# A hybrid pooling and HGRN2 layer on one core: channel-major prompt tokens, broadcast roots, projection banks in turn from two pools, and later final stores

## The chip, the cores and the metric

The kernel runs on one NeuronCore of a Trainium2 chip. The core has a matrix engine (TensorE, PE in the profile; its weight loads are the row PEld), a vector engine (VectorE, DVE), an engine for activations, copies and casts (ScalarE, ACT), a general engine (GpSimd, POOL) and a queue engine (SyncE, SP) that issues most of the transfers. Each engine runs its own instructions in order, and semaphores order the engines against each other. The matrix engine writes into PSUM, eight banks of 128 rows by 512 float32 values; everything else lies in SBUF, 128 partitions wide. Sixteen transfer engines move data between the chip's memory and SBUF.

The metric is the device time of one execution in microseconds (us). Three runs of the kernel before had a median of 2188.99 us.

## The reference

One layer of a streaming encoder is computed for two groups of requests with the same weights: 2048 new tokens (the prompt) and 32 tokens of a running stream (the sample), each of 1024 channels. In short, with B = 1:

```python
h = rmsnorm(x, g_pre_mix)                  # x * rsqrt(mean(x*x) + 1e-6) * g, over 1024 channels
z = h @ w_in                               # 1024 -> 2560
u, zq, zf, zi, zg = split(z, 5 x 512)
y_pool = windows of u over 2/4/8/16 frames, minus u, times w_pool per group, times pool_scale
q, f = silu(zq), lb + (1 - lb) * sigmoid(zf)
o, S1 = hgrn_run(S0, q, k=(1 - lb) * sigmoid(-zf), v=zi, log(f))   # 4 heads of 128, per token exact
y_hg = rmsnorm(o, g_hg_norm) * silu(zg)
x = x + rmsnorm(concat(y_pool, y_hg) @ w_out, g_post_mix)
h2 = rmsnorm(x, g_pre_ffn)
x = x + rmsnorm((silu(h2 @ w_gate) * (h2 @ w_up)) @ w_down, g_post_ffn)   # 2816 hidden
```

It returns the new x of both groups, the last 15 pooling inputs and the last matrix states. All inputs are float32. The kernel keeps nearly that precision by writing an operand as a rounded high part and a rest (hi and lo) and adding three products: hi*hi, hi*lo and lo*hi.

## The kernel before

The prompt is worked in two halves of 1024 tokens (A, then B; B also carries the 32 sample tokens). A half is two blocks of 512 tokens (`tg` 0 and 1), and a block is four tiles of 128 tokens. Per half the order on TensorE, written out by hand (`manual_schedule` for PE), is:

- `values`: the 512 value columns of `w_in` for each token block, 8 channel tiles x 4 token tiles x 3 products of 512 columns, so 96 products a block
- `head_products`: for each of four heads the columns f, q and g, each for the two blocks of 512 tokens, 24 products a block; behind them as background tasks the recurrence (`hgrn`)
- `pool_products`: four pooling groups
- `project`: `w_out`, for each block two column halves (`dh`), each into four PSUM banks
- `gate_up`: gate and up products in a seven-product scheme, results written to memory as hi and lo (`hd`)

Behind both halves follows `down`: six groups of hidden columns, each over eight units (half, token position), each unit seven products out of tiles that SP fetches from `hd` one unit ahead, summed into `acc`.

The other engines' instructions are ordered by a planner that knows estimated durations. Background tasks (`Task`) are advanced by `poll`, which is called between products and compares each task's due time with a running count of estimated TensorE time (`Pace`). Weights come through a stream: `want` lists them, `ahead` loads raw tiles (two items in front) and splits them into hi and lo (`split`: ACT casts, DVE subtracts), `take` hands out the next.

SBUF tiles come from two rotating pools, 39 tiles of 4 KB a partition and 22 of 2 KB; PSUM has a pool `mm` of four banks and a pool `ax` of four.

The places around the change:

- **Input.** `body` loads the first two token tiles, a block of constants and five small vectors (as rows, turned by one transpose, lines 102 to 131). `front_norm` loads token tiles (128 tokens x 1024 channels), forms the mean square on ACT (`sumsq`), the root on POOL (`rstd_of`, line 295, with `pow`), scales the tile on DVE (lines 459 and 469), and `to_channels` (lines 306 to 326) transposes each 128 x 128 piece on TensorE into an `ax` bank, from which ACT writes hi and DVE lo of `hT`. For A's first block this runs per pair of token tiles. For B it starts while A's `gate_up` ends.
- **Projection.** Each `dh` takes three `mm` banks and one `ax` bank (line 875). DVE multiplies them by the gain and ACT sums their squares. Meanwhile `post` of the block before works on the result: residual, second norm, transposes by `to_raw` (line 328) in `ax` banks, and forms on ACT and DVE.
- **Final stores.** In the last group of `down`, a finished token tile is scaled, then an accumulating transfer issued by POOL adds the residual (line 1397), and SP stores the tile (line 1398); this store is put at least six slots (products of one unit and position) after the accumulating transfer in the program. The last unit's two tiles are added on DVE instead and stored by lines 1392 and 1393, on SP and, for the last piece, ACT's queue.

## Time and profile before

| what | value |
|---|---|
| median of three runs | 2188.99 us (2187.97 to 2190.52) |
| the profiled execution | 2187.68 us |
| its span, first to last instruction | 2185.9 us |
| mean granted TensorE clock | 0.997 |
| TensorE busy | 2143.7 us, 98% of the span |
| DVE, ACT, POOL busy | 1414.3, 817.5 and 282.4 us |
| moved by transfers | 315.13 MB, 144 GB/s |

The profile is of one execution. A row of busy time names the line of the kernel, the engine, the operation, the tiles written and read, and the count; "L184" is the helper that issues every ordinary matmul. The table of waits gives who waited, for whom, the total in us, how often, and the longest. The table of stretches gives, for each interval of the span, every engine's busy time with its instructions in brackets, the share of the clock granted to TensorE (1.00 is full), the mean busy share of the 16 transfer engines (it can exceed 1 where packets of several queues overlap), and GB/s. A row of the timeline starts with start and duration; a bracket at its end says how long the engine had been idle and what ended that. Matmuls overlap in the pipeline, so the distance between their starts, not their duration, is what one costs.

### The profile page before, as it was taken

What the parts mean: (1) busy time and instruction counts of PE and PEld (TensorE: products, weight loads), DVE (VectorE), ACT (ScalarE), POOL (GpSimd) and SP (SyncE); (2) the same over time, 40 slices, a digit from 0 to 9 for tenths busy, and PEclk for the clock granted to TensorE, in tenths of its full rate; (3) what the DMA queues carried; (4) which work ended last, traced back from release to release, by engine and by line L of the source; (5) the groups of instructions that cost most, each with busy time, mean ns of one, the idle gap of its engine ahead of it and who ended that gap; (6) DMA issues with size and microseconds to landing.
All of it is one profiled execution on the core that took longest, in us unless ns stands there. A gap on an engine that the chain in (4) does not pass through costs nothing.

```text
span 2185.9 us, 34308 instructions
## 1 busy us (share of the span) xinstructions
PE 2143.7 (98%) x13293; PEld 1712.5 (78%) x13293; DVE 1414.3 (65%) x2309; ACT 817.5 (37%) x1586; POOL 282.4 (13%) x383
## 2 busy tenths in 40 slices
PE   7999999999999999999999999999999999999996
PEld 5878878788888888777777778888888777877785
DVE  6356665697776778365574687766666756566585
ACT  6233234554444456132323564444444521011032
POOL 1033201100000001023220120000000210110033
PEclk9999999999999999999999999999999999999999
DMA  6110043425555558111014524544454797777789
GB/s 221 39 31 21 21 145 131 149 82 169 162 148 151 155 164 268 43 44 34 15 32 146 180 86 125 159 141 140 135 145 140 228 327 200 220 223 206 203 226 308
DMA packets 385179, 315.13 MB, mean 144 GB/s; under 512 B 15701, under 2 KB 318058, under 8 KB 385017
## 3 DMA queue, kind: packets, MB, share of 16 engines
q1 hardware_dynamic: 382856, 305.34, 46.0%
q0 software_dynamic: 2016, 7.34, 1.7%
q8 instruction: 105, 1.72, 0.3%
q14 instruction: 58, 0.47, 0.1%
q10 hardware_dynamic: 144, 0.26, 0.0%
HBM read 214.51 MB, written 98.37 MB: 143 GB/s over the span
## 4 chain that ended last, share of the span: by engine, by line
PE 43%; DVE 3%; DMA 2%; ACT 1%; POOL 1%; issue 0%; SPq 0%; DVEq 0%; POOLq 0%; ACTq 0%
PE gx L184 10%; PE dx L184 10%; PE gy L184 6%; PE dy L184 5%; PE ops L184 4%; PE dz L184 2%; PE gz L184 2%; PE mmb L184 1%; DMA hst<-hdTrue 1%; PE gsps L184 1%; DVE acc L1360 1%; PE gw L184 1%; PE sacc L184 0%; PE zps L184 0%; PE pps L184 0%
## 5 line engine op out<-in xcount | busy, mean ns | idle before, releaser
L184 PE MATMUL gx<-fhi,wf 128*128 128x512 f32 x1376 | 448.5, 394 | 0.0
L184 PEld LDWEIGHTS gx<-fhi,wf 128*128 128x128 f32 x1376 | 258.7, 188 | 59.2 <-issue 1.0
L184 PE MATMUL gx<-flo,wf 128*128 128x512 f32 x688 | 270.1, 393 | 0.0
L184 PE MATMUL gy<-fhi,wf 128*128 128x512 f32 x704 | 234.0, 394 | 0.0
L184 PE MATMUL mmb<-hThi,whi 128*128 128x512 f32 x512 | 219.0, 428 | 0.0
L184 PE MATMUL dx<-dhi,hst 128*128 128x512 f32 x640 | 213.5, 394 | 0.5 <-DVE acc L1360 0.4
L184 PE MATMUL mmb<-hThi,wlo 128*128 128x512 f32 x512 | 201.4, 393 | 0.0
L184 PE MATMUL mmb<-hTlo,whi 128*128 128x512 f32 x512 | 201.2, 393 | 0.0
L1360 DVE TENSOR_TENSOR acc<-dx,acc 128x512 f32<-128x512 f32 x168 | 115.2, 689 | 77.9 <-PE dx L184 77.3
L1094 DVE TENSOR_TENSOR wf<-s,wf 128x512 fp32r<-128x512 f32 x176 | 120.5, 688 | 66.1 <-ACT wf L1089 63.5
L184 PEld LDWEIGHTS gy<-fhi,wf 128*128 128x128 f32 x704 | 132.3, 188 | 30.6 <-issue 0.5
L184 PEld LDWEIGHTS gx<-flo,wf 128*128 128x128 f32 x688 | 129.6, 188 | 28.3
L1089 ACT CAST wf<-s 128x512 fp32r<-128x512 f32 x176 | 108.4, 621 | 105.4 <-PE gy L184 34.7
L184 PEld LDWEIGHTS dx<-dhi,hst 128*128 128x128 f32 x640 | 120.8, 189 | 32.2 <-issue 3.6
L184 PE MATMUL gy<-flo,wf 128*128 128x512 f32 x352 | 138.2, 392 | 0.0
L184 PE MATMUL dx<-dlo,hst 128*128 128x512 f32 x320 | 125.9, 394 | 0.0
L1094 DVE TENSOR_TENSOR wf<-wraw,wf 128x512 fp32r<-128x512 f32 x132 | 89.7, 687 | 50.9 <-ACT wf L1089 50.8
L184 PE MATMUL dy<-dhi,hst 128*128 128x512 f32 x320 | 113.1, 394 | 4.8 <-DMA hst<-hdTrue 4.4
L184 PEld LDWEIGHTS mmb<-hThi,whi 128*128 128x128 f32 x512 | 96.3, 188 | 25.0 <-issue 6.4
L1089 ACT CAST wf<-wraw 128x512 fp32r<-128x512 f32 x132 | 80.9, 620 | 88.3 <-PE gz L184 23.8
L184 PEld LDWEIGHTS mmb<-hThi,wlo 128*128 128x128 f32 x512 | 96.1, 188 | 22.3
L184 PEld LDWEIGHTS mmb<-hTlo,whi 128*128 128x128 f32 x512 | 96.7, 189 | 18.3 <-issue 2.6
(312 smaller groups left out, 4115.1 us busy)
## 6 DMA issues: line engine op xcount, KB each, us to landing
hst<-hdFalse SPq DMA_DIRECT2D x140, 256.0 KB, 2.9
hst<-hdTrue SPq DMA_DIRECT2D x140, 256.0 KB, 3.4
wraw<-in_w_gate_dram SPq DMA_DIRECT2D x50, 512.0 KB, 4.0
wraw<-in_w_up_dram SPq DMA_DIRECT2D x50, 512.0 KB, 3.9
hdFalse<-hhi SPq DMA_DIRECT2D x77, 256.0 KB, 2.6
hdFalse<-hlo SPq DMA_DIRECT2D x77, 256.0 KB, 2.5
hdTrue<-hhi SPq DMA_DIRECT2D x77, 256.0 KB, 2.4
hdTrue<-hlo SPq DMA_DIRECT2D x77, 256.0 KB, 3.1
```

The source lines that it names most:

```text
L184: nc.tensor.matmul(out, l, r, start=start, stop=stop, skip_group_check=more)
L1089: nc.scalar.copy(wf[:, 0], getattr(M, src) if isinstance(src, str) else src)
L1094: nc.vector.tensor_tensor(wf[:, 1], getattr(M, src) if isinstance(src, str) else src, wf[:, 0].bitcast(F32), ALU.subtract)
L1360: nc.vector.tensor_tensor(dst, ps, dst, ALU.add)
```

## The change

The prompt is given to the kernel a second time, channel-major (`x_channels`, 1024 x 2048), prepared with the inputs. The five small vectors become 32 more columns of the constants, loaded alone on ACT's queue.

**Input, half A** (`first_values`, all engines in program order): channel tiles are loaded beside the weights. The first block's value products use unnormed channels (times the gain, as hi and lo), and the results are multiplied by each token's root afterwards. For the second block, token tiles are loaded only for the statistics; the roots of 128 tokens, put on a diagonal by POOL, are multiplied by a matrix of ones on TensorE, which gives a bank that holds each token's root in all partitions; DVE multiplies gain and roots into the channel tile, ACT writes hi, DVE lo (`scaled_channels`). The first block's `hT` is made in the same way at the end of `first_values`. The heads of A then take the second block first, and the first head works f and q block by block.

**Input, half B**: the mean squares come from token halves loaded during A's heads (`later_stats`), and channel tiles are scaled as above. Nothing is transposed at the input but the 32 sample tokens.

**Projection**: the first column half takes all its banks from `mm`, the second from `ax`; the transposes of `to_raw` use the pool that the projection does not (`turned`). B's second block keeps one bank of the other pool for the sample.

**Stores**: 14 slots of distance instead of 6.

```diff
-                for ap, r0, n in ((ins["g_pre_mix"], 0, 8), (ins["g_pre_ffn"], 8, 8), (ins["pool_scale"], 16, 4),
-                                  (ins["lb_logits"], 20, 8), (ins["g_hg_norm"], 28, 1)):
-                    nc.sync.dma_start(out=rows[r0:r0 + n, :], in_=ap.rearrange("a (k p) -> (a k) p", p=P))
+        nc.scalar.dma_start(out=cons[:, C_VEC:C_END], in_=cst[:, C_VEC:C_END])
...
+        x_t = ins["x_channels"].rearrange("(k p) t -> p k t", p=P)
...
+        nc.gpsimd.memset(ones, 1.0)
...
-        def to_channels(tiles, dst, gcol, col0, seen=None, which=()):
...
-                ps = axbank("tps")
+                ps = turned[0]("tps")
...
+            S.blocks = [(0, 512), (512, 1024)] if B else [(512, 1024), (0, 512)]
...
+        def channel_load(S, tg, k, n):
+            t0 = S.tok0 + tg * 512
+            nc.sync.dma_start(out=S.xT[tg][k // 2][:, k % 2:k % 2 + n], in_=x_t[:, k:k + n, t0:t0 + 512])
+
+        def token_tiles(S, tg):
+            S.xt[tg] = [ztile("xt", [P, D]) for _ in range(4)]
+            for i, xt in enumerate(S.xt[tg]):
                 r0 = S.tok0 + (tg * 4 + i) * P
                 nc.sync.dma_start(out=xt, in_=x_p[r0:r0 + P, :])
-                xs.append((xt, P))
-            if S.B and tg == 1:
+
+        def token_stats(S, tg):
+
+            S.rs[tg], S.dg[tg] = [], t2("dg", [P, 4, P])
+            for i, xt in enumerate(S.xt[tg]):
+                st = new_stat()
+                sumsq(xt, P, st[:, 0:1])
+                S.rs[tg].append(rstd_of(st, P))
+                nc.gpsimd.tensor_scalar(S.dg[tg][:, i], ident, S.rs[tg][i], None, ALU.mult)
+            S.xt[tg] = None
+
+        def later_stats(S):
+
+            st = S.st
+            for i in range(NCH):
+                for c in range(2):
+                    x = t2("xtl")
+                    r0 = S.tok0 + i * P
+                    nc.sync.dma_start(out=x, in_=x_p[r0:r0 + P, c * 512:c * 512 + 512])
+                    sumsq(x, P, st[:, 2 * i + c:2 * i + c + 1])
+                    del x
+                yield 20000.0
+            ev = st[:, 0:16].rearrange("p (i c) -> p i c", c=2)
+            nc.gpsimd.tensor_tensor(st[:, 16:24], ev[:, :, 0], ev[:, :, 1], ALU.add)
+            nc.gpsimd.tensor_scalar(st[:, 16:24], st[:, 16:24], 1.0 / D, EPS, ALU.mult, ALU.add)
+            nc.gpsimd.tensor_tensor(st[:, 24:32], st[:, 16:24], nhalf[:, 0:1].broadcast_to([P, NCH]), ALU.pow)
+            S.rs = [[st[:, 24 + 4 * tg + i:25 + 4 * tg + i] for i in range(4)] for tg in range(2)]
+
+        def scaled_channels(S, tg):
+            rb = axbank("rb")
+            for i in range(4):
+                mm(rb[:, i * P:(i + 1) * P], ones, S.dg[tg][:, i], True, True, 112.0)
+            if S.hT is None:
+                S.hT = [(xtile(f"hThi{k}"), xtile(f"hTlo{k}")) for k in range(KD)]
+            cs = slice(tg * 512, tg * 512 + 512)
+            yield 0.0
+            for k in range(0, KD, 2):
+                x = S.xT[tg][k // 2]
+                for i in range(2):
+                    nc.vector.scalar_tensor_tensor(x[:, i], x[:, i], g_pre[:, k + i:k + i + 1], rb, ALU.mult, ALU.mult)
+                    nc.scalar.copy(S.hT[k + i][0][:, cs], x[:, i])
+                for i in range(2):
+                    hi, lo = (t[:, cs] for t in S.hT[k + i])
+                    nc.vector.tensor_tensor(lo, x[:, i], hi.bitcast(F32), ALU.subtract)
+                S.seen[tg] = k + 2
+                if S.B and tg == 0 and k >= 4:
+                    ahead(Stream.used + k // 2 - 1)
+                yield 5000.0 if S.B and tg == 0 else 2800.0
+
...
+        def front_norm(S, tg):
...
+            channel_tiles(S, tg)
+            S.dg[tg] = t2("dg", [P, 4, P])
+            for i in range(4):
+                nc.gpsimd.tensor_scalar(S.dg[tg][:, i], ident, S.rs[tg][i], None, ALU.mult)
...
+            yield from scaled_channels(S, tg)
...
+        def first_values(S):
+
+
+            front_loads(S)
+            S.xT[0] = [ztile("xT", [P, 2, 512]) for _ in range(4)]
+            for kp in range(4):
+                channel_load(S, 0, 2 * kp, 2 if kp else 1)
+                raws(kp + 1)
+                if kp == 0:
+                    channel_load(S, 0, 1, 1)
+            nc.sync.dma_start(out=cons[:, 0:C_VEC], in_=cst[:, 0:C_VEC])
+            xg = {}
+
+            def unscaled(k):
+                x, c = S.xT[0][k // 2][:, k % 2], xtile("xg", [P, 2, 512])
+                nc.scalar.activation(c[:, 0], x, AF.Copy, scale=g_pre[:, k:k + 1])
+                nc.vector.scalar_tensor_tensor(c[:, 1], x, g_pre[:, k:k + 1], c[:, 0].bitcast(F32), ALU.mult, ALU.subtract)
+                xg[k] = c[:, 0], c[:, 1]
+
+            token_tiles(S, 1)
+            S.xT[1] = [ztile("xT", [P, 2, 512]) for _ in range(4)]
+            for kp in range(4):
+                channel_load(S, 1, 2 * kp, 2)
+                raws(kp + 5)
+            token_tiles(S, 0)
+            unscaled(0)
+            ahead(1)
+            unscaled(1)
+            pss = value_tiles(S)
+            for k in range(0, KD, 2):
+                _, hi, lo = take(0)
+                if k + 2 < KD:
+                    unscaled(k + 2)
+                    ahead(Stream.used + 1)
+                    unscaled(k + 3)
+                else:
+                    ahead(Stream.used + 1)
+                if k == 4:
+                    token_stats(S, 1)
+                for kk in range(2):
+                    ah, al = xg.pop(k + kk)
+                    for i in range(4):
+                        value_products(pss, i, ah, al, i * P, hi[kk], lo[kk], k + kk == 0, k + kk == KD - 1)
+                    if k + kk == KD - 3:
+                        later = scaled_channels(S, 1)
+                        next(later)
+                        next(later)
+            for i in range(4):
+                (nc.vector.tensor_copy if i % 2 else nc.scalar.copy)(S.vt[i], pss[i])
+            pss = value_tiles(S)
+            for k in range(0, KD, 2):
+                _, hi, lo = take(0)
+                next(later, 0)
+                ahead(Stream.used + 1)
+                if k == 2:
+                    next(later, 0)
+                elif k == 4:
+                    token_stats(S, 0)
+                    gate_bounds()
+                elif k == 6:
+                    for i in range(4):
+                        if i % 2:
+                            nc.vector.tensor_scalar(S.vt[i], S.vt[i], S.rs[0][i], None, ALU.mult)
+                        else:
+                            nc.scalar.activation(S.vt[i], S.vt[i], AF.Copy, scale=S.rs[0][i])
+                for kk in range(2):
+                    if k + kk == KD - 1:
+                        earlier = scaled_channels(S, 0)
+                        next(earlier)
+                    ah, al = S.hT[k + kk]
+                    for i in range(4):
+                        value_products(pss, i, ah, al, (4 + i) * P, hi[kk], lo[kk], k + kk == 0, k + kk == KD - 1)
+            for i in range(4):
+                (nc.vector.tensor_copy if i % 2 else nc.scalar.copy)(S.vt[4 + i], pss[i])
+            for _ in earlier:
+                pass
+
...
+            if h == 0 and not S.B:
+                wf, wq = take(), take()
+                for blk in S.blocks:
+                    blocks_of(wf, use_f, [blk])
+                    blocks_of(wq, use_q, [blk])
+            else:
+                H.smp = [tile_of(use_f), tile_of(use_q)]
...
-                pss = [mmbank("ops") for _ in range(3)] + [axbank("ops")]
-                sps = axbank("osps") if smp else None
+                own, other = (axbank, mmbank) if dh else (mmbank, axbank)
+                turned[0] = other
+                pss = [own("ops") for _ in range(3)] + [(other if smp and dh else own)("ops")]
+                sps = other("osps") if smp else None
...
-                    stores.append((slot[0] + 6, lambda: nc.sync.dma_start(out=outs[0][0, rows, :], in_=f)))
+                    stores.append((slot[0] + 14, lambda: nc.sync.dma_start(out=outs[0][0, rows, :], in_=f)))
...
+        with tc.manual_schedule(engines=set(mybir.EngineType) - {mybir.EngineType.Unassigned}):
+            first_values(halves[0])
         with tc.manual_schedule(engines={mybir.EngineType.PE}):
-            start_norms(halves[0])
+            late_constants()
...
+                    halves[1].st = CP.tile([P, 32], F32, name="st_b")
+                    Task(later_stats(halves[1]), 5000.0)
...
+    arrays["x_channels"] = np.ascontiguousarray(inputs["x_prompt"][0].T)
```

194 lines of the change are left out of this document (69 added, 125 removed).

## The prediction

> **What bounds the kernel now.** I read the page's busy times first, then the waits of TensorE, then stretches of 20 us.
>
> ```profile
> span 2185.9 us, 34308 instructions
> PE 2143.7 (98%) x13293; PEld 1712.5 (78%) x13293; DVE 1414.3 (65%) x2309; ACT 817.5 (37%) x1586; POOL 282.4 (13%) x383
> ```
>
> TensorE is the bound: 42 us of the span are idle. So a change can win only by taking matmuls away, by filling those 42 us, or by removing time in which the clock is low. The stretches say where they are:
>
> ```profile
> 0.00:20.00 20.00, 6.41 (x21) 4.38 (x22) 8.55 (x25) 9.66 (x18) 3.01 (x10) 1.00 0.90 324
> 380.00:400.00 20.00, 17.71 (x71) 13.93 (x70) 13.34 (x19) 10.63 (x21) 1.66 (x4) 0.91 0.40 107
> 840.00:860.00 20.00, 20.00 (x104) 16.55 (x103) 17.50 (x25) 15.82 (x27) 6.33 (x10) 1.00 1.05 349
> 2120.00:2140.00 20.00, 19.82 (x87) 15.90 (x85) 14.92 (x23) 6.51 (x18) 9.04 (x17) 1.00 1.05 283
> 2140.00:2160.00 20.00, 14.31 (x53) 10.99 (x54) 9.94 (x16) 2.90 (x8) 6.28 (x11) 0.91 1.05 338
> 2160.00:2180.00 20.00, 14.50 (x62) 11.22 (x61) 14.56 (x22) 5.79 (x16) 10.94 (x17) 1.00 1.03 296
> ```
>
> Columns: stretch, length, busy us (with instructions) of PE, PEld, DVE, ACT, POOL, then granted clock, DMA share, GB/s. The start loses 13.6 us, one place in the first half's output projection 2.3, the last two stretches 11.2, some of it behind the last product. The waits name the causes:
>
> ```profile
> PE vps L130 <- DMA rows<-in_g_hg_norm_dram: 8.1, 1, 8.1
> PE dy L184 <- DMA hst<-hdTrue: 4.4, 2, 4.2
> PE ops L184 <- ACT junk L288: 3.5, 2, 2.3
> ```
>
> The first is the input path that is rewritten, the second the transfers of the last group, the third the projection's banks. The change touches all three.
>
> **Term 1, the start of the first half.** Today the first value product stands behind a norm and transposes:
>
> ```profile
> 4.41 1.06 ACT L288 ACTIVATE junk<-xt 128x1024 bf16<-128x1024 f32 x1 [2.40 <-DMA xt<-in_x_prompt_dram]
> ...
> 14.34 0.79 PE L184 MATMUL vps<-whw,hThi 128*128 128x512 f32 x1 [3.15 <-ACT whw L221]
> ...
> 18.34 0.63 PE L184 MATMUL vps<-wlw,hThi 128*128 128x512 f32 x1
> 18.77 0.62 PE L184 MATMUL vps<-whw,hTlo 128*128 128x512 f32 x1
> ...
> 49.89 0.39 PE L184 MATMUL vps<-whw,hThi 128*128 128x512 f32 x1
> ...
> 69.98 0.39 PE L184 MATMUL vps<-whw,hThi 128*128 128x512 f32 x1
> 70.67 0.39 PE L184 MATMUL mmb<-hThi,whi 128*128 128x512 f32 x1
> ```
>
> The head products start at 70.67. From 49.89 to 69.98 lie 29 triples, so a product costs 20.09/87 = 0.231 us; the 192 value products of a half cost 44.3. At 18.34 to 18.77 one still costs 0.43.
>
> New start: 512 KB had landed by 4.41, which is what channel tile 0 and half the first weight pair weigh, both first on SP. Casting and splitting them takes one ACT step each, then a DVE step:
>
> ```profile
> L227 ACT CAST whi<-wraw 128x512 fp32r<-128x512 f32 x64 | 36.5, 622 | 0.2 <-DMA wraw<-in_w_in_dram 0.2
> L320 ACT ACTIVATE hThi<-tps,vec x40: 466/687/700, 11.2 to 861.4; 128x512 fp32r<-128x512 f32 x24, 128x256 fp32r<-128x256 f32 x16
> L321 DVE SCALAR_TENSOR_TENSOR hTlo<-tps,vec,hThi x40: 474/730/754, 11.8 to 862.6; 128x512 fp32r<-128x512 f32 x24, 128x256 fp32r<-128x256 f32 x16
> ```
>
> The channel cast runs before 4.4; weight high part to 5.0, low part (about the 0.7 of a DVE step) to 5.7. The 32 constants now come alone on ACT's queue, a form the trace lacks. Nearest are the norm rows, whose last landing released TensorE at 8.05, so the start lies between 5.0 and 8; I take 5.7, since nothing stands ahead of it there.
>
> A cold clock costs about 8 products at 0.43 instead of 0.23, 1.6 us. The roots need eight fp32 products of 128 columns; two records make one (va takes 32 products in a half pair and has 64 records):
>
> ```profile
> 131.09 0.61 PE L184 MATMUL ops<-va,attn 128*128 128x128 f32 x4
> 131.53 0.39 PE L184 MATMUL ops<-S,qa 128*128 128x128 f32 x2
> 131.76 0.39 PE L184 MATMUL ops<-vb,attn 128*128 128x128 f32 x2
> ```
>
> That is 0.22 us each, 1.8. Sum: 5.7 + 1.6 + 44.3 + 1.8 = 53.4, plus 0.4 for the cache transposes, which now follow. For waits I add 1.5, between none and 5. Two places can wait. TensorE reaches the first broadcast at about 24 us (72 products in) and there needs the statistics of the second token block, behind 6.45 MB of loads (its engine runs in order, so all later products stand behind such a wait); 324 GB/s over the first 20 us is 6.5 MB, so they land at 20, and a square sum (1.06), the root and the POOL scaling end at about 22.5. At the hand-over, DVE still has to make the first token block: 8 x (0.73 + 0.69) = 11.4 us, behind 48 products that need only the second block, 11.1 us. Heads start at 55.3: **gain 15.4**, bounds 9 and 17.
>
> **Term 2, the second half.** 64 transposes go and eight broadcasts come.
>
> ```profile
> 43.87 0.60 PE L314 MATMUL tps<-cons,xt 128*128 128x128 f32 x4
> 44.22 0.48 PE L184 MATMUL vps<-whw,hThi 128*128 128x512 f32 x1
> ...
> 45.00 0.60 PE L314 MATMUL tps<-cons,xt 128*128 128x128 f32 x4
> ```
>
> Four transposes and three products take 1.13 us; less 0.69 that leaves 0.44 a group, 7.0 for 16 groups, against 1.8 + 0.2: **gain 5.0**, bounds 0 and 5.0. It counts in full because TensorE idles nowhere at 840 to 860. DVE is the cover: per block it makes 8 x (0.73 + 0.69) = 11.4 instead of 4 x 0.75 + 8 x 0.73 = 8.8 (a scaled token tile is 0.75 in this trace):
>
> ```profile
> L469 DVE TENSOR_SCALAR xt<-xt,st x12: 744/754/1596, 30.7 to 851.4; 128x1024 f32<-128x1024 f32 x12
> ```
>
> It is busy 17.5 of 20 us there, so 2.6 us more a block just fits. The square sums move to the first half's heads with 16 loads of 256 KB, where ACT has room; SP's queue carries them (a rival below). I cost them at nothing.
>
> **Term 3, banks in turn.** Now three of four banks of a projection half are those of the half before, so its products wait for evictions behind the forms on DVE and ACT.
>
> ```profile
> 380.00:384.00 4.00, 1.89 (x9) 1.18 (x7) 4.00 (x7) 1.81 (x4) 0.00 (x0) 1.00 1.16 316
> 384.00:388.00 4.00, 3.82 (x10) 3.00 (x11) 3.09 (x4) 3.97 (x11) 1.05 (x4) 0.57 0.79 214
> 388.00:392.00 4.00, 4.00 (x19) 3.29 (x18) 2.47 (x5) 2.06 (x4) 0.61 (x1) 1.00 0.00 0
> ```
>
> The two waits are 3.5 us. Behind the longer, the clock is 0.57 and 10 records run instead of 19: 8 x 0.23 = 1.8 us. With separate pools both go, 5.3 together; lower end 0, if the other pool's banks, now used by the transposes, are as late. I take **4.5**, near the upper end, as four banks come free a whole projection half earlier. The Trainium skill (TensorE: Matmul & The Clock Gate, Part 1: The HAM clock gate) says the clock halves after an idle window of about 3.4 us. By that the 2.3 us here would cost no clock and the term would be at most 3.5; the row with 0.57 disagrees, and I go by the row.
>
> **Term 4, stores later.** A store waits on SP for its accumulating load, and all fetches stand behind it.
>
> ```profile
> SPq L1398 <- DMA acc<-x1d: 36.7, 9, 9.0
> ```
> ```profile
> 2090.99 8.59 SPq L1340 DMA_DIRECT2D hst<-hdFalse  x7
> 2108.60 0.34 SPq L1398 DMA_DIRECT2D out_dram<-acc  x1
> ...
> 2159.86 19.98 SPq L1398 DMA_DIRECT2D out_dram<-acc  x6
> 2179.94 1.76 SPq L1393 DMA_DIRECT2D out_dram<-acc  x3
> ```
> ```profile
> 2100.00:2104.00 4.00, 4.00 (x18) 3.06 (x17) 2.80 (x5) 0.81 (x3) 2.99 (x5) 1.00 0.25 80
> 2104.00:2108.00 4.00, 4.00 (x19) 3.23 (x18) 3.29 (x6) 2.06 (x6) 1.28 (x4) 1.00 0.90 139
> ...
> 2172.00:2176.00 4.00, 2.89 (x12) 2.00 (x12) 2.29 (x5) 1.73 (x5) 3.71 (x6) 1.00 1.06 237
> ```
>
> Eight slots more of delay (11 us at 1.4 a slot of six products) end most of the 36.7 us. But the engines' share is 1.03 to 1.05 from 2120 to 2180: the transfers are the limit there, and an order does not make them fewer. What comes back is the time in which they idled because SP stood: 3.0 + 0.4 us at 2100 to 2108 and some at the end, **4**. Upper end 8: the 35 records missing of 88 at 2140 to 2160. Lower end -4: four stores instead of two stand ahead of the last outputs, 1 MB at 296 GB/s is 3.5 us. The Trainium skill (DMA: Bandwidth & Descriptors, Issuing engines are not separate DMA queues) says that transfers interleave on the same 16 engines whoever issues them, which the shares above 1 bear out; by it the term is the 4, without it the 8.
>
> **The sum.** 15.4 + 5.0 + 4.5 + 4 = 28.9 us. The profiled execution took 2187.68 (1.8 beside its span), so 2158.8; the median shown lies 1.3 higher, at 2188.99: **2160 us**.
>
> **The rivals.** (a) The split of the second head weight lands on DVE behind the 16 steps of the hand-over: two evictions, the 16 steps and the split's two take 1.4 + 11.4 + 1.4 = 14.2 us on DVE where the 24 products ahead of it give 5.5, so 8.7 us of wait: 2168.7. For it: that work comes earlier in the program; against: DVE idles in the microseconds before, and the planner may pull the split there. (b) The last group is freed wholly, +4: 2156; against it the shares above 1. (c) The end gets longer by its lower bound, -4 instead of +4: 2168. For it: 19.98 us in which SP already waits at the final stores. (d) Slower than before: the 16 added loads take tiles from the pool of 22 that the head products use for splits; a load that waits for a tile holds every weight load behind it on SP. Weights are asked for two items of 48 products (22 us) ahead, so it decides only when eight load pairs each hold SP longer than that cover by about 4 us: 32 us lost, 2192. Against it: DMA and ACT are little used there. (e) The start doesn't come forward: tokens or channel tiles come so late that TensorE waits 10 us more at the first broadcast, 2170; the 6.5 MB in 20 us speak against it.
>
> **How the numbers follow.** Forecast 0.52; (a) 0.15, (b) 0.12, (c) 0.10, (e) 0.07, (d) 0.04. The forecast's own range lets the four terms miss independently: towards their lower ends by 6.4, 5.0, 4.5 and 8 us, whose root of squares is 12, towards the upper by 1.6, 0, 0.8 and 4, which makes 4.4: 2156 to 2172. The rivals (a), (b), (c) and (e) lie within it; what they do together with a missed term is given 4 to 6 us more on each side, and (d) is left out: 2150 to 2176. No change means within 0.2% (4.4 us), about what this kernel's measurement can tell. All cases but (d) are faster by more, and a sum of several mishaps gets some chance: 0.93 faster, 0.03 same, 0.04 slower.
>
> **What would show it.** Right: the first value product before 6 us, heads at 53 to 58, no L288 wait before the projection's products, no clock of 0.57 near 380, L1398's wait on SP far below 36.7 us while the DMA share stays near 1 to the end. Wrong: a TensorE wait for a weight split or a broadcast before 70 us, a wait on SP for a tile among the head products, or a tail after the last product longer than now (TensorE is busy 2.89 us of the stretch from 2172, so the last product ends near 2174.9, 11.0 before the span).

## The result and the profile after

The changed kernel takes **2164.23 us** (median of 4 runs, 2163.60 to 2164.81). The kernel before, run beside it on the same chip, takes 2189.76 (4 runs, 2187.97 to 2190.73). The ratio is 0.9884, with a 95% interval of 0.987 to 0.9897: 25.5 us less. The forecast was 2160, the range 2150 to 2176. The profiled execution after took 2164.81 and its span is 2163.0, 22.9 us less than the span profiled before; the rest of the 25.5 comes from the choice of executions: the one profiled before, 2187.68, lay below all four timed, and the one profiled after is the slowest of its four. One execution of a later run, the profiled one of the input part alone, ran at a granted clock of 0.752 for 2616.82 us; its time and its trace are left out below.

The span and the busy times of the page of the changed kernel:

```profile
span 2163.0 us, 34223 instructions
PE 2131.1 (99%) x13196; PEld 1701.0 (79%) x13196; DVE 1426.9 (66%) x2321; ACT 822.5 (38%) x1604; POOL 288.6 (13%) x391
```

TensorE now idles 31.9 us of the span instead of 42.2. That is 10 of the 22.9 us; the other 13 are work that is gone or runs faster (transposes, products at a low clock). The same stretches of 20 us as before (stretch, length, busy us of PE, PEld, DVE, ACT and POOL, granted clock, transfer share, GB/s):

```profile
0.00:20.00 20.00, 12.92 (x43) 10.02 (x44) 10.50 (x17) 14.41 (x24) 2.87 (x13) 1.00 0.92 347
...
380.00:400.00 20.00, 20.00 (x88) 16.31 (x87) 8.03 (x13) 7.24 (x16) 5.22 (x10) 1.00 0.61 178
...
840.00:860.00 20.00, 20.00 (x95) 15.15 (x94) 13.43 (x20) 8.88 (x15) 0.00 (x0) 1.00 0.91 268
...
2120.00:2140.00 20.00, 17.23 (x74) 13.19 (x73) 13.74 (x21) 5.79 (x16) 7.76 (x15) 1.00 1.06 295
2140.00:2160.00 20.00, 9.13 (x36) 6.33 (x36) 10.00 (x17) 2.89 (x8) 8.71 (x11) 0.83 1.04 354
```

The start loses 7.1 us instead of 13.6, the place near 380 nothing, and at 840 to 860 DVE has room. The last two stretches lose 13.6 us, some 9 of it behind the last product. The two longest waits of TensorE:

```profile
PE vps L173 <- ACT whw L210: 7.0, 1, 7.0
PE dx L173 <- DMA hst<-hdTrue: 4.2, 3, 1.6
```

The wait for the parameter rows (8.1) and the one before the projection's products (3.5) are gone, and the one for the last group's transfers has stayed. The first products, and the hand-over to the heads (start, us, engine, line, operation, and in brackets the idle time before it with its releaser):

```profile
6.99 0.79 PE L173 MATMUL vps<-whw,xg 128*128 128x512 f32 x1 [6.99 <-ACT whw L210]
...
13.16 0.41 PE L173 MATMUL vps<-wlw,xg 128*128 128x512 f32 x1
```
```profile
52.68 0.83 PE L173 MATMUL rb<-dg,ones 128*128 128x128 f32 x6
54.62 0.49 PE L173 MATMUL rb<-dg,ones 128*128 128x128 f32 x2 [1.12 <-POOL dg L426]
...
58.12 0.50 PE L173 MATMUL mmb<-hThi,whi 128*128 128x512 f32 x1
```

The times at which the first product of each stage starts, from the views by tile, give the account by stage (us; a stage ends where the next begins; the last group is counted from the last sample product to the start of the last product):

```
stage                           before            after             change
start to the first head product 0 to 70.7         0 to 58.1         -12.6
heads, first half               70.7 to 309.1     58.1 to 297.3     +0.8
projection, first half          309.1 to 407.4    297.3 to 391.5    -4.1
gate and up, first half         407.4 to 841.5    391.5 to 822.9    -2.7
values, second half             841.5 to 892.7    822.9 to 871.9    -2.2
heads, second half              892.7 to 1155.9   871.9 to 1134.9   -0.2
projection, second half         1155.9 to 1257.4  1134.9 to 1234.9  -1.5
gate and up, second half        1257.4 to 1725.6  1234.9 to 1702.3  -0.8
down products to last group     1725.6 to 2073.7  1702.3 to 2052.4  +2.0
last group                      2073.7 to 2174.5  2052.4 to 2150.5  -2.7
behind the last product         2174.5 to 2185.9  2150.5 to 2163.0  +1.1
```

So by the prediction's terms: the start 12.6 instead of 15.4; the second half's input 4.9 (it falls in gate and up of the first half and in the values of the second) as forecast at 5.0; the banks 5.6 instead of 4.5; the later stores, which show in the last two rows, 1.6 instead of 4. And 2.0 us are lost in a stage that no term spoke of, the down products ahead of the last group.

At the end the wait of SP for the accumulating loads did shrink from 36.7, but others have grown, and the transfers are over 1 as before (waits of SP's queue: us in total, times, longest; then two stretches of 8 us):

```profile
SPq L1490 <- DMA acc<-x1d: 17.8, 5, 6.3
SPq L1490 <- DMA hst<-hdTrue: 10.5, 7, 2.8
...
SPq L1352 <- DVE fgs L1351: 4.3, 2, 4.0
```
```profile
2120.00:2128.00 8.00, 8.00 (x37) 6.49 (x36) 5.87 (x9) 2.38 (x7) 3.16 (x7) 1.00 1.06 311
...
2144.00:2152.00 8.00, 5.13 (x21) 3.28 (x19) 3.61 (x7) 2.35 (x7) 5.27 (x7) 1.00 1.07 305
```

### The profile page after: what moved, and what is told of

Its sections match the earlier page's. It is cut to its first block, busy times and chain, and to the rows that moved or that the text cites. A ratio compares the mean times of both kernels' runs of the same rounds, so it can differ in the third digit from the quotient of the medians.

```text
span 2163.0 us, 34223 instructions
## 1 busy us (share of the span) xinstructions
PE 2131.1 (99%) x13196; PEld 1701.0 (79%) x13196; DVE 1426.9 (66%) x2321; ACT 822.5 (38%) x1604; POOL 288.6 (13%) x391
## 3 DMA queue, kind: packets, MB, share of 16 engines
q0 software_dynamic: 2016, 7.34, 1.7%
## 4 chain that ended last, share of the span: by engine, by line
PE 87%; DVE 4%; DMA 2%; ACT 2%; issue 1%; POOL 1%; SPq 0%; DVEq 0%; POOLq 0%; ACTq 0%
PE gx L173 21%; PE mmb L173 15%; PE gy L173 11%; PE dx L173 9%; PE ops L173 9%; PE gz L173 5%; PE dy L173 5%; PE dz L173 2%; PE vps L173 2%; DMA hst<-hdTrue 2%; PE gb L173 1%; PE gw L173 1%; PE gsps L173 1%; PE ups L173 1%; DVE acc L1452 1%
```

## The experiments

The theory is the prediction's: four terms, each with its own cause. The rivals: one change of the three carries the gain of another, the start is set by something other than the loads and the split, and the end is limited not by the transfers but by the order on SP. Each run below was timed in five rounds beside the kernel before, whose median stood between 2189.2 and 2189.6 in the three comparisons.

**The parts alone.** First the banks, on the kernel before:

```diff
-                pss = [mmbank("ops") for _ in range(3)] + [axbank("ops")]
+                own, other = (axbank, mmbank) if dh else (mmbank, axbank)
+                pss = [own("ops") for _ in range(3)] + [(other if smp and dh else own)("ops")]
```

> The kernel before with the projection's banks in turn from two pools and nothing else. Theory (term 3 was a wait for banks plus the low clock behind it): the 3.5 us of TensorE waits on L288 go, the granted clock stays at 1.00 through the first half's projection, and the time falls by 4 to 6 us, as the stage from the first product of the projection to the first of gate and up is shorter by 4.1 us in half A and 1.5 us in half B in the changed kernel. Rival (those stages got shorter because the input change moved the work around them): under 2 us.

Measured 2183.52, ratio 0.9969 (0.9958 to 0.998): 6.1 us less. The stretches where the kernel before had TensorE busy for 1.89 and 3.82 us, the second with 10 records and a clock of 0.57:

```profile
380.00:384.00 4.00, 4.00 (x19) 3.25 (x18) 4.00 (x6) 1.77 (x4) 0.19 (x1) 1.00 1.02 302
384.00:388.00 4.00, 4.00 (x19) 3.25 (x19) 3.08 (x4) 4.00 (x10) 1.29 (x3) 1.00 0.79 222
```

Both are full. The projection of the first half lasts 94.1 us instead of 98.3 and that of the second 99.9 instead of 101.5: 5.8 us, where the waits alone would have been 3.5 (2.3 in the first half's projection, 1.2 in the second's). Most of the rest is the clock, as the term had it: behind the wait of 2.3, nine products took 3.75 us (384.18 to 387.93) where nine at 0.231 take 2.1, and 2.3 + 1.7 are 4.0 of the first half's 4.2.

Then the stores, on the kernel before:

```diff
-                    stores.append((slot[0] + 6, lambda: ...
+                    stores.append((slot[0] + 14, lambda: ...
```

> The kernel before with the final stores at 14 slots and nothing else. Theory (the 16 transfer engines are the limit of the last group, and an order does not make the bytes fewer): within 2 us of the kernel before, the DMA share still above 1 from some 20 us into the last group to the end, and the waits of TensorE on fetched tiles moved towards the end, not gone. Rival (SP's queue behind its stores was the limit): 6 to 10 us faster.

Measured 2188.65, ratio 0.9992 (0.9984 to 1.0001): 1.0 us less, not to be told from nothing. The down products up to the last one are 1.8 us shorter and what follows it is 1.5 longer, 12.9 instead of 11.4. The longer end need not come from the stores: with the banks alone, and the stores at six slots, 12.7 us follow the last product.

The same step taken back on the changed kernel:

```diff
-                    stores.append((slot[0] + 14, lambda: ...
+                    stores.append((slot[0] + 6, lambda: ...
```

> The changed kernel with the output stores six slots behind their accumulating loads, as before the change, instead of fourteen. On the kernel before, fourteen slots gave 1.0 us, within the noise. If the transfers are the limit in the last group whatever stands on SP: 2164 to 2166, the last product at most 2 us later, the wait of SP at the stores back above 30 us. Rival: the later stores are worth more here because the accumulating loads land later (9.0 us, SP's order counts): 2168, the prediction's 4 us.

Measured 2166.83, ratio 0.9896 (0.9881 to 0.991), 2.6 us above the changed kernel, and the two intervals overlap. The wait is back:

```profile
SPq L1490 <- DMA acc<-x1d: 37.7, 8, 8.9
```

Its last group takes 99.7 us where that of the changed kernel takes 98.1, and what follows the last product is the same, 12.6 and 12.5. Twenty microseconds of SP's waiting are worth 1.0 us on the one kernel and 2.6 on the other by the medians, and 1.6 both by these stages and by the last two rows of the account by stage. That is on the side of the limit by transfers; the prediction's 4 is reached in neither kernel.

Last, the input part alone: the changed kernel with the banks and the stores as they were (both edits above, reversed).

> The changed kernel with the banks of the projection from one pool and the stores six slots behind, as before the change: the input part alone. The banks alone gave 6.1 us on the kernel before, the stores 1.0, all three parts 25.5. If the parts are independent, this gives 25.5 - 6.1 - 1.0 = 18.4: 2171. The first and second half's starts alone (12.6 and 4.9 by the first products of the stages) give 17.5: 2172. Rival: the three parts share a gain (the banks wait less when the sum of squares of the second half is not in their way): 2168 or less, with the first gate product earlier than 395.5.

Measured 2171.9 (four runs, 2170.2 to 2172.9), ratio 0.9917 (0.9903 to 0.9931): 17.3 us below the kernel before. 17.3 + 6.1 + 1.0 is 24.4 of the 25.5, and 26.0 with the 2.6 for the stores. The parts are independent as closely as this can be measured.

**The start: table and statistics.** ACT's first operations in the changed kernel:

```profile
0.72 0.41 ACTq L107 DMA_DIRECT2D cons<-shape_constants  x1
4.41 1.28 ACT L529 ACT_TABLE_LOAD   x1 [4.41 <-DMA xT<-x_channels]
5.71 0.72 ACT L529 ACTIVATE xg<-xT,cons 128x512 fp32r<-128x512 f32 x1
6.34 1.12 ACT L210 CAST whw<-wrow 128x512 fp32r<-128x512 f32 x2
```

The table load stands behind the first transfer, though it needs no data of it. In the kernel before, it did not:

```profile
0.73 1.28 ACT L288 ACT_TABLE_LOAD   x1 [0.73 <-PEq L1549]
```

There the first activation waited for one transfer only, until 4.41. In the changed kernel it waits for two, the channel tile and the 32 constants, and one of the two waits is an instruction of its own (an EVENT_SEMAPHORE of L529, 4.4 us) that stands ahead of the load. The edit gives ACT a small operation on data that is there from the beginning, and moves the statistics of the first token block two weight pairs forward:

```diff
         nc.gpsimd.memset(nhalf, -0.5)
+        early = CP.tile([P, 4], F32, name="early")
+        nc.scalar.activation(early, nhalf, AF.Copy)
...
+                if k == 0:
+                    token_stats(S, 0)
-                if k == 2:
+                elif k == 2:
                     next(later, 0)
                 elif k == 4:
-                    token_stats(S, 0)
                     gate_bounds()
```

> The changed kernel with two moves in its first values: a four-column copy on ACT ahead of everything, so that the load of the activation table (1.28 us, at 4.41 in the changed kernel, behind the first channel tile) runs while the first transfers are on their way; and the statistics of the first token block two channel pairs earlier. Theory: first product at 5.7 instead of 6.99 us, no 1.12 us wait for the diagonal at 54.62, heads at 55.7 instead of 58.12, so 2.4 us off the changed kernel, 2161.8. Rival (the loads of the first pair set the pace, so the start moves and the next products wait): under 1 us.

Measured 2162.91, ratio 0.9875 (0.9861 to 0.9888): 1.3 us below the changed kernel, within the overlap of the two intervals. In the trace both steps work:

```profile
1.16 1.28 ACT L137 ACT_TABLE_LOAD   x1 [1.16 <-PEq L1646]
2.46 0.20 ACT L137 ACTIVATE early<-nhalf 128x4 f32<-128x4 f32 x1
4.77 0.72 ACT L531 ACTIVATE xg<-xT,cons 128x512 fp32r<-128x512 f32 x1 [2.11 <-DMA cons<-shape_constants]
```

The first activation comes 0.94 us earlier, not 1.28: now the 32 constants are what it waits for. The first product starts at 6.06, the wait for dg is gone, and the heads begin at 55.36, 2.76 earlier. In the profiled execution nearly all of that is given back: 1.2 us in the heads of the first half (1.0 of it waits that the trace puts down to no releaser) and 1.3 behind the last product.

**The start: the clock.** The first 13 products of the changed kernel take 6.17 us (6.99 to 13.16), 0.47 each with two short waits, where later ones take 0.23. In the run just shown they are slow from 6.06 to about 10.1 only:

```profile
9.66 0.63 PE L175 MATMUL vps<-wlw,xg 128*128 128x512 f32 x1
10.09 0.70 PE L175 MATMUL vps<-whw,xg 128*128 128x512 f32 x2
10.63 0.40 PE L175 MATMUL vps<-wlw,xg 128*128 128x512 f32 x1
```

The edit puts ten products that nobody reads ahead of them, on top of the edit above:

```diff
             front_loads(S)
+            cold = axbank("cold")
+            for _ in range(10):
+                mm(cold[:, 0:P], ones, ones, True, True, 0.0)
```

> The changed kernel with the early activation and the early statistics of the run before (2162.9 us there), and with ten fp32 products of a 128 x 128 tile of ones ahead of the first value product; their bank is read by nobody. In the changed kernel the first 13 products stand 0.43 us apart until 13.2 us, in the run before until 10.1. Theory: TensorE is granted its full clock only some us after it began to work, so ten products from about 2 us on bring the full clock to the first value product or shortly behind it: about nine products at 0.23 instead of 0.43 us, heads at 53.5 to 54.5 instead of 55.4, and the time about 1.5 us below the run before. Rival 1: the low clock has nothing to do with what ran before (first weights, waits): products stay at 0.43 us for 4 us, no gain. Rival 2: the ten products end after 6 us and push the first value product back: heads at 55.4 or later.

Measured **2160.46**, ratio 0.9864 (0.9849 to 0.9878): the fastest of all, 3.8 us below the changed kernel. The two intervals still overlap, but each of its four runs (2158.5 to 2161.2) lies below each of the changed kernel's four.

```profile
1.02 4.64 PE L175 MATMUL cold<-ones 128*128 128x128 f32 x20 [1.02 <-POOL cmps L144]
5.91 0.59 PE L175 MATMUL vps<-whw,xg 128*128 128x512 f32 x1 [0.25 <-ACT whw L212]
6.79 0.50 PE L175 MATMUL vps<-wlw,xg 128*128 128x512 f32 x1 [0.29 <-DVE wlw L213]
7.13 0.62 PE L175 MATMUL vps<-whw,xg 128*128 128x512 f32 x2
```

The ten products run in the time in which TensorE waited anyway, and from 7.13 on a product takes 0.23. So the slow start is a matter of how long TensorE has been at work, and rival 1 of that run falls. The gain at the heads is 1.0 us against the run before (54.4 against 55.4).

**The hand-over.** The prediction named 48 products of the second token block as the cover for the 16 steps of the first. With the first head's products tile by tile there are only 24:

```diff
-            if h == 0 and not S.B:
-                wf, wq = take(), take()
-                for blk in S.blocks:
-                    blocks_of(wf, use_f, [blk])
-                    blocks_of(wq, use_q, [blk])
-            else:
-                H.smp = [tile_of(use_f), tile_of(use_q)]
+            H.smp = [tile_of(use_f), tile_of(use_q)]
```

> The changed kernel with the first head's products tile by tile (f on both token blocks, then q) instead of block by block. At the hand-over (58.1 us) DVE still has to make the 16 steps of the first token block. By the prediction's working that needs the cover of 48 products (11.1 us): with only 24 (5.5 us) ahead, TensorE reaches the first block's channels at about 63.6 and waits about 3 us in all for the pairs, which would appear some 4.2, 7.1, 9.9 and 12.8 us behind the hand-over: 2167 us, first w_out product 3 us later than 297.3. Rival: the evictions of the values and the pairs are early enough, or the wait is given back in the heads stage, whose end is set elsewhere: 2164, first w_out product within 1 us of 297.3.

Measured 2169.32, ratio 0.9905 (0.989 to 0.992): 5.1 us above the changed kernel by the medians, with single runs from 2166.5 to 2171.8; the two intervals just overlap, but each run lies above each of the changed kernel's four. The waits appear in the first head, 9.6 to 12.7 us behind its first product (57.09), at the last two of the four places expected:

```profile
66.72 0.50 PE L173 MATMUL mmb<-hThi,whi 128*128 128x512 f32 x1 [0.33 <-ACT hThi L458]
...
69.76 0.50 PE L173 MATMUL mmb<-hTlo,whi 128*128 128x512 f32 x1 [0.51 <-DVE hTlo L461]
```

There are four of them, 1.6 us together where 3 were expected, and the heads of the first half last 241.7 instead of 239.2: 2.5 us in the profiled execution, which was the fastest of its runs. The cover is needed; what the slower runs lose beside it has no view.

**The end: the accumulating transfer.** The kernel adds the residual of 14 of the 16 last tiles in the transfer itself, on POOL's queue (q0), and nearly all the rest goes by q1 (transfers by queue from 2080 to 2163 us of the changed kernel: packets, MB, share of the 16 engines' time):

```profile
q1 hardware_dynamic: 7007, 16.38, 53.7%
q0 software_dynamic: 2016, 7.34, 44.7%
```

Those 7.34 MB take 44.7% of 83 us, 37 us of the engines, 5.0 us for each MB; q1's 16.38 MB take 44.6 us, 2.7 for each MB. (A share above 1 doesn't need two queues: at 840 to 860 of the kernel before, where it was 1.05, q0 had nothing to move.) Three runs take that transfer away in three ways. In the first the residual is loaded and DVE adds it, for all eight units of the last group, as the kernel already does for the last one, but with the scaling four slots behind as for the others:

```diff
-                        half_done(t, 0, n + 1 == len(units))
+                        half_done(t, 0, direct_of(n))
```

with direct_of true for the last eight units; the other three calls alike. The product with the gain, which DVE made in its scaling step, goes to POOL, and each half of a tile is stored as soon as DVE has made it.

> The changed kernel, but in all eight units of the last group the residual is loaded into a tile of its own (512 KB) and added on DVE in the same step that scales by the root, where the accumulating transfer read both the tile and the residual and wrote the tile; the gain goes to POOL. Theory (transfer engines are the limit of the last group): 14 accumulating transfers, 31.2% of the engines' 120 us in the last part, give way to plain loads of the same bytes; the DMA share falls below 1 for part of the group, TensorE's waits of about 5 us there go, and the end comes 5 to 10 us earlier. Rival (what counts is SP's program order or DVE): no gain, or a loss, as 14 more loads now stand on SP between the fetches.

Measured 2171.15, ratio 0.9909 (0.9894 to 0.9924): 7 us slower than the changed kernel. The transfers have room, yet TensorE now waits for DVE, DVE for POOL (13.6 us in its scaling step, 3.7 in the changed kernel) and SP for DVE:

```profile
2080.00:2088.00 8.00, 6.74 (x30) 5.17 (x28) 6.47 (x8) 0.81 (x3) 5.73 (x8) 1.00 0.41 140
```
```profile
PE dx L173 <- DVE acc L1452: 8.2, 10, 2.2
```
```profile
SPq L1488 <- DVE acc L1487: 51.2, 24, 9.8
```

In the second the distance is longer, on top of the early activation and statistics: the scaling ten slots behind instead of four, and the stores four slots behind that. (The last two of these stores aren't issued in this kernel, so the rows of two tiles aren't written out: 1 MB less than the others move.)

> The changed kernel with the early activation and early statistics (2162.9 us alone) and with the residual of the last group loaded and added on VectorE instead of accumulated by the transfer, this time with VectorE's scaling ten slots behind its statistics instead of four and the store four slots behind that. With four slots and the stores at once it was 7 us slower than the changed kernel, with SP 51.2 us in waits for VectorE at the stores and TensorE 11 us for VectorE. Theory: the transfers' load is what the accumulation costs, and the loss came from the order of POOL, VectorE and SP alone: with the distance gone, TensorE waits for neither, the share of the transfers falls below 1, the last product comes 3 to 6 us earlier: 2156 to 2160. Rival: VectorE itself has no room (the additions of the last group plus these): TensorE still waits for VectorE by over 5 us, 2166 to 2172.

Measured 2167.53, ratio 0.9896 (0.988 to 0.9913): 4.6 us slower than with the early steps alone, though it moves less. SP's wait for DVE at the stores is down, and TensorE waits for DVE as long as in the run before:

```profile
PE dx L175 <- DVE acc L1455: 8.2, 9, 2.2
```
```profile
SPq L1496 <- DVE acc L1490: 19.8, 9, 7.4
```

So the order of the stores was not what held TensorE. In the third way, DVE's order stays as it is, and POOL adds:

```diff
-                    nc.gpsimd.dma_start(out=f, in_=x1d[rows, :], accum_op=ALU.add)
+                    for ds in (slice(0, 512), slice(512, D)):
+                        nc.gpsimd.tensor_tensor(f[:, ds], f[:, ds], xh[:, ds], ALU.add)
```

with the load of xh for every tile at its first half.

> The changed kernel with the accumulating transfer of the last group taken away without touching VectorE's order: SP loads the residual of every tile into a tile of its own when the tile's first half is done, POOL adds it in two steps behind VectorE's scaling, and the store stays fourteen slots behind. In the two runs with VectorE adding the residual the transfers had room (share 0.4 to 1.0) but TensorE waited for VectorE, which waited for POOL. Theory: in the last group an accumulating 512 KB costs the transfers much more than a plain load (11.7 us from issue to landing for the next fetch, against 5.0 us without it), so the share falls below 1 in places, the waits for hst go, and TensorE, which owes nothing to POOL's additions, finishes the last product 3 to 7 us earlier: 2157 to 2161. Rival: POOL with 2.6 us more per tile falls behind (its statistics are what VectorE's scaling waits for), VectorE waits for it and TensorE for VectorE: 2166 to 2172.

Measured 2178.55, ratio 0.9948 (0.9935 to 0.9962): 14 us slower than the changed kernel, and 6 above the range of the rival. Here are DVE's scaling step of the changed kernel, POOL's additions in this one, and DVE's scaling step and additions in this one, all in the last group (line, engine, operation, shapes, count, busy us, mean ns):

```profile
L1487 DVE SCALAR_TENSOR_TENSOR acc<-acc,st,gv 128x512 f32<-128x512 f32 x28 | 20.3, 743 | 3.7 <-POOL st L292 3.7
```
```profile
L1490 POOL TENSOR_TENSOR acc<-acc,x1r 128x512 f32<-128x512 f32 x28 | 38.9, 1389 | 15.0 <-DVE acc L1487 14.9
```
```profile
L1487 DVE SCALAR_TENSOR_TENSOR acc<-acc,st,gv 128x512 f32<-128x512 f32 x28 | 32.9, 1194 | 12.1 <-POOL st L292 12.1
L1452 DVE TENSOR_TENSOR acc<-dx,acc 128x512 f32<-128x512 f32 x36 | 24.1, 685 | 6.4 <-PE dx L173 5.6
```

The same instruction takes 1194 ns instead of 743 while POOL adds: 28 of them, 12.6 us of DVE. The addition of a product from its bank keeps its 685 ns, the mean of the changed kernel too. The Trainium skill (SBUF — State Buffer, SBUF: two separate sides) says that VectorE with two inputs from SBUF and a GpSimd operation that reads SBUF hold one pair of ports in turn, each for a whole instruction; the two rows agree, since the scaling reads two tiles from SBUF and the addition one tile and a bank. The trace doesn't show the ports.

The two runs before show the same lengthening. There POOL multiplies by the gain in 31 operations of 1314 and 1336 ns, and DVE's step, which now adds the residual, takes 1028 and 1008 ns; the first of them:

```profile
L1487 DVE SCALAR_TENSOR_TENSOR acc<-acc,st,x1r 128x512 f32<-128x512 f32 x31 | 31.5, 1028 | 13.6 <-POOL st L292 13.6
```

DVE's waits for POOL's roots before this step are 13.6, 12.6 and 12.1 us in the three runs, against 3.7. So none of the three takes the accumulating transfer away alone: each puts 28 or more operations of some 1.3 us on POOL beside DVE. What the transfer itself costs in time isn't shown.

The third way, joined with the early activation, the early statistics and the warming products:

> The run before joined with the early activation, the early statistics and the ten products that warm the clock (2160.5 us without POOL's additions). If the parts add: 3.8 us below the run before, 2153 to 2157. If POOL's additions cost time, 2162 to 2168.

Measured 2173.71, ratio 0.9924 (0.991 to 0.9937): 4.8 us below the run before. The second case of the expectation, with a time 6 us above its range, and at the same time a second look at what the early steps and the warm clock give: 3.8 us without POOL's additions, 4.8 with them.

## Why the prediction was right, and where it was off

**Term 1, the start (15.4 forecast, 12.6 measured).** The mechanism held: the first products need one channel tile, half a weight pair and two steps each. Two amounts were off and one wait was elsewhere. The first product came at 6.99 instead of 5.7, since the step "the channel cast runs before 4.4" left out ACT's table load: before, it lay in a time in which ACT waited for its data anyway; now it stands behind the first channel tile. With the load out of the way the cast still starts only at 4.77, behind the constants. The cold clock was put at 1.6 us, 8 products at 0.2 more; 13 products were slow, 6.17 us where 13 x 0.231 is 3.0, so 3.2, some 0.6 of it in the two short waits. The wait allowed for was 1.5, and the one that came was 1.1, at the broadcast of the first token block (54.62), neither at the first broadcast nor at the hand-over, the two places named. Sum by these: 6.99 + 3.2 + 44.3 + 1.8 + 0.4 + 1.1 = 57.8 against 58.1.

**The first rival**, the split of the second head weight behind 16 DVE steps, didn't come: TensorE doesn't wait between 58 and 98 us. The prediction's reason against it held in the trace, where the planner had made that split at 50 to 55 us. Its larger neighbour, the cover by 48 products, is real: with 24 the kernel loses 2.5 to 5 us.

**Term 2, the second half (5.0 forecast, 4.9 measured).** The 0.44 us per group of four transposes, less the eight broadcasts, came out. The 16 added loads cost no more than that: the stage in which they run, the heads of the first half, changed by +0.8 us, so the rival that put the total above that of before falls.

**Term 3, the banks (4.5 forecast, 5.6 in the whole, 6.1 alone).** The two rows had given 5.3 and that was the right sum; the deduction for the other pool's banks being late was not needed. The 1.8 us for the low clock behind a wait of 2.3 are borne out by the nine products that took 1.7 us too long (384.18 to 387.93): without them no more than 3.5 were to be had.

**Term 4, the stores (4 forecast, 1.6 by stage, 1.0 and 2.6 by the runs).** The mechanism held and its size was off. "What comes back is the time in which they idled because SP stood": here are the stretches of the transfers' idle time, first of the kernel before, then of the one after, each at the same distance behind the last sample product:

```profile
2088.00:2096.00 8.00, 8.00 (x36) 6.54 (x35) 7.75 (x12) 0.72 (x2) 1.47 (x2) 1.00 0.69 216
2096.00:2104.00 8.00, 8.00 (x36) 6.30 (x35) 6.63 (x11) 2.17 (x6) 4.46 (x7) 1.00 0.51 134
```
```profile
2067.00:2075.00 8.00, 8.00 (x37) 6.49 (x36) 7.75 (x12) 0.72 (x2) 1.48 (x2) 1.00 0.71 202
2075.00:2083.00 8.00, 8.00 (x36) 6.43 (x35) 6.65 (x11) 2.17 (x6) 4.49 (x7) 1.00 0.65 196
```

Before, 8 x (0.31 + 0.49) = 6.4 us go unused in them, after 8 x (0.29 + 0.35) = 5.1. So 1.3 us came back and not 3.4. Between the two kernels that differ in the stores alone it is 1.8: with six slots in the changed kernel the shares of these stretches are 0.66 and 0.48, and 6.9 us go unused. The rest stays idle for another reason: in the two stretches of the changed kernel SP's waits are for TensorE alone, for products to free the tiles that it fetches into (L1432 and L1343 for PE, 10.8 us in 12 waits of at most 1.0), where in the kernel before it stood 9.0 us in one wait for the first accumulating load. The sample's store at L1352, 4.0 us for DVE, comes behind these stretches, from 2085.5 to 2089.5. From 2112 before and from 2088 after the share is at about 1 until the last product. The time behind the last product grew from 11.4 to 12.5, but the rival with the longer end isn't shown by that: with the stores at six slots it is 12.6 in the changed kernel and 12.7 in the kernel before with the banks alone.

**What no term had.** The down products ahead of the last group take 350.1 us instead of 348.1, with no more waits. Each product is a little longer (count: shortest, median and longest ns, first and last start), first before, then after; by the distance of the starts, which is what one costs, 1427 products in this stage stand 229.6 ns apart before and 231.1 after, 2.2 us in all:

```profile
L184 PE MATMUL dx<-dlo,hst x320: 387/390/629, 1769.7 to 2174.3; 128*128 128x512 f32 x160
```
```profile
L173 PE MATMUL dx<-dlo,hst x320: 387/395/398, 1746.4 to 2150.3; 128*128 128x512 f32 x160
```

The nine kernels with the new input that are shown here have 349.7 to 350.8 us there (393 to 395 ns, 230.8 to 231.2 apart), the two others without it 347.7 and 348.3 (392 and 390 ns, 229.3 and 229.5 apart). So these 2 us go with the input part, though they lie far behind it: the products are the same, and TensorE's waits in this stage agree to 0.2 us.

**The sum.** 28.9 was forecast from the profiled execution, and the spans give 22.9: 12.6 + 4.9 + 5.6 + 1.6, less the 2.0 in the down products, and 0.2 gained together in the heads of both halves and in gate and up of the second. The medians say 25.5. Against the forecast the start lacks 2.8, the stores 2.4 and the down products 2.0, and the banks give 1.1 more; by the profiled executions the forecast misses by 6.0 us (2158.8 against 2164.81). That the medians lie only 4.2 us from it is luck: the forecast was counted from a profiled execution that was a quick one.

**The signs.** Of those named for being right, four came: no L288 wait, no clock of 0.57 near 380, SP's wait for the accumulating loads down from 36.7 to 17.8 us, and a share near 1 to the end. The first product (6.99 instead of before 6) and the heads (58.12 instead of 53 to 58) came later than named. Two signs of being wrong came as well, both small: the wait of 1.1 us at a broadcast before 70 us, and the end that is 1.1 us longer.

What isn't settled: what makes the down products 0.6% longer with the new input (where its tiles lie in memory was not varied), and why the time behind the start differs by some 3 us between runs of one kernel, so that the early steps' 2.8 us at the heads are 1.3 in the median.

## What to carry to other kernels

When a start is moved forward, list what every engine has to do once before its first real operation (a table, a first transfer, a cold clock): what lay under a wait lies on the path as soon as the wait goes, and cheap early operations on data that is there anyway take it off again (3.8 us here, to 2160.46). Products that wait for banks pay twice, for the wait and for the clock behind it, and taking turns between two pools cost nothing. Where the transfers' share is over 1, a later store gives back only the idle time that no other wait on its queue keeps (1.6 us of 20 us of SP's waiting). Before moving the transfers' work to another engine, look at what runs beside it: here POOL's additions made VectorE's scaling step 1194 ns instead of 743, and the kernel 14 us slower.

## What the runs showed of the hardware

The low speed at the start isn't in the column of the granted clock. From 8 to 12 us the changed kernel and the one with the warming products show 1.00 alike, with 10 and 19 records:

```profile
8.00:12.00 4.00, 4.00 (x10) 3.13 (x11) 4.00 (x7) 3.45 (x7) 0.00 (x0) 1.00 1.05 406
```
```profile
8.00:12.00 4.00, 4.00 (x19) 3.21 (x19) 2.47 (x5) 3.09 (x5) 0.00 (x0) 1.00 1.05 398
```

So at the start the clock is read from the distance of the products. From TensorE's first operation to full speed it took 6.2 us in the changed kernel, 4.0 with the early activation and between 5.8 and 6.1 with the warming products. The Trainium skill (TensorE: Matmul & The Clock Gate, Part 1: The HAM clock gate) says that full speed comes after one busy window of some 3.4 us, and that the windows run freely. An estimate from that page's window is a time between one and two windows, 3.4 to 6.8 us, depending on where the first product falls; all three agree with it.

A DVE step with two tiles as inputs takes 1194 instead of 743 ns beside POOL's additions, and an accumulating transfer costs the engines 5.0 us for each MB against 2.7 for the others in the same stretch. What the second is worth in time stays open: the runs without it had the transfers below 1 for long, but all of them put more work on POOL beside DVE, and were slower.
